# Scaling and turning the first four value heads on VectorE instead of TensorE and ScalarE

## The chip, the cores and the metric

The kernel runs on one core of a Trainium2 chip. The metric is the device time of one execution in microseconds (us), as a median of several runs. The engines are called PE (TensorE matmul), DVE (VectorE), ACT (ScalarE), POOL (GpSimd) and SP (SyncE, which here only issues DMAs). L405 means line 405 of the kernel before.

## The reference

One layer of a streaming encoder, in fp32, on 512 new prompt frames and 64 new sample frames (T = 576 rows in all). What matters here is its first stage: a norm, one wide projection, and the value heads that come out of it.

```python
hn = rmsnorm(x, g_norm1)                    # every row divided by its root mean square
proj = hn @ w_in                            # (576, 2048) @ (2048, 6144)
q, k, v, gb, gc, hc = jnp.split(proj, ...)  # 8 heads x 128 each for q, k, v; 1024 conv channels each for gb, gc, hc
...
o_attn = stick_breaking_blocks(q, k_all, v_all, P)
u = gc * hc                                 # then a convolution of width 3, times gb
...
x = x + mix @ w_out
x = x + (silu(h2 @ w_gate) * (h2 @ w_up)) @ w_down
```

`v` is an output too (`v_prompt`, `v_sample`), with the frame as row and the channel as column.

## The kernel before

**Layout.** All activations are kept with the channel on the 128 partitions and the 576 frames along the free axis. The row norm of `x` is not applied to `x`: the products run on `x * g_norm1`, and each result is multiplied later by `R1`, a [128, 576] tile that holds the factor of every frame, the same in all partitions. The same factors stand once more in `rst`, a [128, 5] tile with the frame on the partition.

**Stages.** First `x` is turned to the channel layout, and the value heads 0 to 3 are computed meanwhile with plain products (`step0`, L691); their sums go, not yet scaled, into the tiles `e0` (heads 0 and 1; names `E00`, `E01`) and `e1` (heads 2 and 3; name `E1`). The end of this is near 68 us. Then stage A does the other 22 units of `w_in`, then come the convolution and attention, the output projection and the feed-forward part.

**Units and products.** From stage A on, a unit is a 2048 x 256 block of a weight. It is done as seven products of half-size blocks (a Strassen-Winograd scheme), numbered 1 to 7; (3, 1) is product 1 of unit 3. A product is 24 matmuls of 128x128 by 128x288 in a row at L405: eight blocks, each with high part times high part, low times high and high times low. In stage A unit 0 and 1 are `gh` (convolution), unit 2 is `qk`, unit 3 is `gb`. PE runs the products in the order of the list `opening`, and then of a loop:

```python
opening = [(0, 1), (0, 2), (1, 1), (0, 3), (0, 6), (1, 2), (0, 5), (0, 7), (1, 3), (0, 4), (1, 6), (2, 1), (1, 5),
           (1, 7), (2, 2), (1, 4), (2, 6), (2, 7), (2, 5)]      # then (3, 1), (2, 3), (2, 4), (3, 2), ...
```

**What a product needs.** The weight block arrives by DMA in `raw_a` or `raw_b` (L328, 1 MB each). DVE forms sums of its quarters in place (L345, L349, L351, L353), ACT rounds the block to its high part (`whl`, L228), and DVE subtracts to get the low part (`whl`, L229). Four `whl` tiles go round, so the split for a product can start only when the product four places earlier is done. The first matmul of a product needs ACT's half, the second needs DVE's. Behind products 1, 5 and 6 ACT keeps a copy of the running sum (`part`, L428), and DVE adds it to another product's sum later (L897, L919, L931).

**Order of the work.** PE runs in the order of the program. DVE, ACT, POOL and SP are ordered by a list scheduler from stage A on, which places the instructions by its own idea of when their inputs are there; on the chip each engine then runs its list strictly in order. A small queue of generators (`pipe`) decides where on PE's list, and how early, the side work is written: one tick passes per three matmuls, and `yield n` puts the rest n ticks later.

**The four heads.** `plain_tokens` (spawned at L975, with lags of 8, 22, 36 and 50 ticks) takes one of the four `E` tiles: PE turns four 128x128 pieces (L790) and the last 64 frames (L798), ACT copies them from PSUM with the factor of `rst` as scale (L793, L800), and SP stores each piece twice, to the output and to `v_dram`, from which attention reads later: four DMAs. The heads 4 and 5 use `tokens` (L804) instead: DVE turns the [128, 576] tile in 32x32 squares in one instruction (L807), and ten DMAs put the pieces, 128 bytes each, into their places (L812, L815). The tiles `tokp`, `toks` and `tok` come from three buffers under the tag `hl`, which `ghs`, `s2` and `yt` use too.

Of the kernel before, what the change touches and what calls it, by code (L numbers as in the profile page):

```python
# [12 lines left out]
AF = mybir.ActivationFunctionType  # L13
ALU = mybir.AluOpType
PSUM = bass.MemoryType.PSUM

P = 128
TP = 512
TS = 64
T = TP + TS  # L20
# [82 lines left out]
def tile_hybrid_stream_step(  # L103
# [6 lines left out]
    nc = tc.nc  # L110
# [6 lines left out]
    kp, vp, ks, vs = k_prompt[0, 0], v_prompt[0, 0], k_sample[0, 0], v_sample[0, 0]  # L117
# [18 lines left out]
    v_dram = tc.dram_tile([NH, T, P], F32, name="v_dram")  # L136
# [4 lines left out]
    def misc(name):  # L141
        return ps_z.tile([P, 512], F32, tag="misc", name=name, bufs=2)
# [75 lines left out]
    pipe = Pipeline()  # L218
# [18 lines left out]
    ident = const.tile([P, P], F32, name="ident")  # L237
# [277 lines left out]
    ssr, rst, nhalf = (vecs[:, o : o + 5] for o in (304, 312, 320))  # L515
# [14 lines left out]
    R1 = None  # L530
# [98 lines left out]
    def hl_tile(name):  # L629
        return tmp.tile([P, 2, HALF], F32, tag="hl", name=name, bufs=3).rearrange("p i t -> p (i t)")  # L630

    LAG = 3
    with tc.manual_schedule(engines={mybir.EngineType.Activation, mybir.EngineType.DVE, mybir.EngineType.SP}):
# [102 lines left out]
        R1 = rpool.tile([P, T], F32, tag="R", name="R1", bufs=2)  # L736
# [48 lines left out]

    def plain_tokens(E, h, lag):
        yield lag
        pa = misc("tok_p")
        for i in range(4):
            nc.tensor.transpose(pa[:, i * P : (i + 1) * P], E[:, i * P : (i + 1) * P], ident)  # L790
        t = hl_tile("tokp")[:, :TP].rearrange("p (i d) -> p i d", d=P)
        for i in range(4):
            nc.scalar.activation(out=t[:, i, :], in_=pa[:, i * P : (i + 1) * P], func=AF.Copy, scale=rst[:, i : i + 1])  # L793
        nc.sync.dma_start(out=vp[:, h, :].rearrange("(i p) d -> p i d", p=P), in_=t)
        nc.sync.dma_start(out=v_dram[h][:TP].rearrange("(i p) d -> p i d", p=P), in_=t)
        yield 3
        pb = misc("tok_q")
        nc.tensor.transpose(pb[:TS, :P], E[:, TP:T], ident)  # L798
        tz = hl_tile("toks")[:TS, :P]
        nc.scalar.activation(out=tz, in_=pb[:TS, :P], func=AF.Copy, scale=rst[:TS, 4:5])  # L800
        nc.sync.dma_start(out=vs[:, h, :], in_=tz)
        nc.sync.dma_start(out=v_dram[h][TP:], in_=tz)

    def tokens(E, dst, dst_s, dram, lag):  # L804
        yield lag
        t = hl_tile("tok")
        nc.vector.transpose(out=t, in_=E)  # L807
        for g in range(0, P, BK):
            rows = t[g : g + BK].rearrange("j (t c) -> j t c", c=BK)
            for b, to in ((TP, dst), (T, dram)):  # L810
                if to is not None:
                    nc.sync.dma_start(out=to[:, g : g + BK].rearrange("(t j) c -> j t c", j=BK),  # L812
                                      in_=rows[:, : b // BK])
        for a in range(TP, T, BK):
            nc.sync.dma_start(out=dst_s[a - TP : a - TP + BK].rearrange("j (g c) -> g j c", c=BK), in_=t[:, a : a + BK])  # L815
# [158 lines left out]
    for E, h, lag in ((e1[0], 2, 8), (e1[1], 3, 22), (e0[0], 0, 36), (e0[1], 1, 50)):  # L974
        pipe.spawn(plain_tokens(E, h, lag))  # L975
# [111 lines left out]
    for h in range(NH):  # L1087
        t = tpool.tile([P, 2, T], F32R, tag=f"t{h}", name=f"mixa{h}")
# [658 lines left out]
```

## Time and the profile before

| | |
|---|---|
| median of 3 runs | 2322.34 us (2322.25 to 2322.53) |
| the profiled execution | 2323.28 us, its span 2321.6 us |
| PE busy | 2310.5 us (100% of the span) |
| DVE busy | 1952.7 us (84%) |
| ACT busy | 1216.2 us (52%) |
| POOL busy | 303.7 us (13%) |
| DMA moved | 368.57 MB, 159 GB/s on average |

Times in the trace count from the start of the span. A timeline row gives the start, the duration, the engine, the line, the operation, out<-in and the count, and in brackets how long the engine had been idle and what ended that. A row's duration is from its start to its end, while the engine starts the next one a little earlier; so what an instruction costs on a busy engine is the step from its start to the next start.

### The profile page before, as it was taken

The numbers are of one execution on the slowest core, as the hardware profiler recorded it, in microseconds if no ns is written. First come the engines' busy times: TensorE is split into PE (matmuls) and PEld (weight loads), VectorE is DVE, ScalarE is ACT, GpSimd is POOL, SyncE is SP. The second block draws the span as 40 slices with busy tenths as digits, with TensorE's granted clock in tenths as the row PEclk, the third lists the DMA queues.
The fourth block names the chain that finished last, engine by engine and source line by source line (L and its number), as shares of the span: only waits on it lengthen the run. The fifth ranks groups of instructions, "written<-read, shape, count | busy, mean of one in ns | idle before, by whom it ended". The sixth has DMA issues, their size and how long they took to land.

```text
span 2321.6 us, 43509 instructions
## 1 busy us (share of the span) xinstructions
PE 2310.5 (100%) x17404; PEld 2303.5 (99%) x17404; DVE 1952.7 (84%) x2878; ACT 1216.2 (52%) x2163; POOL 303.7 (13%) x374
## 2 busy tenths in 40 slices
PE   9999999999999999999999999999999999999999
PEld 8999999999999999999999999999999999999999
DVE  8889989897778898888888888888888777987897
ACT  8556656455787554444444444444444444444443
POOL 0212121110332320000000000000000002431222
PEclk9999999999999999999999999999999999999999
DMA  8444343546754554544444444344344936885654
GB/s 273 134 121 130 89 145 101 153 122 208 194 142 120 179 189 127 158 149 129 155 130 150 141 139 155 119 152 152 121 155 136 351 129 208 226 242 186 207 128 109
DMA packets 544762, 368.57 MB, mean 159 GB/s; under 512 B 84918, under 2 KB 528976, under 8 KB 544560
## 3 DMA queue, kind: packets, MB, share of 16 engines
q1 hardware_dynamic: 538064, 356.42, 49.2%
q0 software_dynamic: 6384, 9.24, 2.3%
q8 instruction: 136, 2.23, 0.4%
q14 instruction: 66, 0.54, 0.1%
q10 hardware_dynamic: 112, 0.14, 0.0%
HBM read 285.52 MB, written 80.23 MB: 158 GB/s over the span
## 4 chain that ended last, share of the span: by engine, by line
PE 94%; DVE 2%; ACT 2%; POOL 1%; DMA 1%; issue 0%; SPq 0%; POOLq 0%; ACTq 0%; DVEq 0%
PE psy L405 47%; PE psw L405 24%; PE psx L405 12%; PE pjo L224 5%; PE pj L691 1%; PE pjz L691 1%; PE psv L405 1%; PE pjm L691 1%; DVE wlo L177 0%; DVE pl L229 0%; PE psx L556 0%; DMA vtok<-v_dram 0%; ACT ph L228 0%; ACT pr L1237 0%; DVE z L1235 0%
## 5 line engine op out<-in xcount | busy, mean ns | idle before, releaser
L229 DVE TENSOR_TENSOR whl<-raw_a,whl 128x1024 fp32r<-128x1024 f32 (+4 forms) x384 | 431.7, 1125 | 55.7 <-ACT whl L228 54.2
L405 PE MATMUL psy<-t,whl 128*128 128x288 f32 x3000 | 447.1, 294 | 0.0
L228 ACT CAST whl<-raw_a 128x1024 fp32r<-128x1024 f32 (+4 forms) x384 | 360.4, 940 | 139.0 <-PE psx L405 42.8
L405 PE MATMUL psy<-h_s,whl 128*128 128x288 f32 x2766 | 416.4, 294 | 0.0
L405 PEld LDWEIGHTS psy<-t,whl 128*128 128x128 f32 x3000 | 414.4, 188 | 0.0
L405 PE MATMUL psw<-t,whl 128*128 128x288 f32 x2688 | 388.9, 294 | 0.0
L405 PEld LDWEIGHTS psy<-h_s,whl 128*128 128x128 f32 x2766 | 383.1, 188 | 0.1
L405 PEld LDWEIGHTS psw<-t,whl 128*128 128x128 f32 x2688 | 366.8, 188 | 0.0
L228 ACT CAST whl<-raw_b 128x1024 fp32r<-128x1024 f32 (+5 forms) x234 | 211.3, 905 | 206.9 <-issue 71.3
L229 DVE TENSOR_TENSOR whl<-raw_b,whl 128x1024 fp32r<-128x1024 f32 (+5 forms) x234 | 252.0, 1077 | 72.9 <-ACT whl L228 72.1
L428 ACT COPY part<-psy 128x288 f32<-128x288 f32 x309 | 122.9, 398 | 340.2 <-PE psy L405 337.8
L405 PE MATMUL psx<-h_s,whl 128*128 128x288 f32 x1164 | 170.2, 294 | 0.0
L228 ACT CAST whl<-s 128x1024 fp32r<-128x1024 f32 (+5 forms) x103 | 95.3, 925 | 123.2 <-PE psw L405 115.6
L405 PEld LDWEIGHTS psx<-h_s,whl 128*128 128x128 f32 x1164 | 159.6, 188 | 0.0
L405 PE MATMUL psy<-t12a,whl 128*128 128x288 f32 x1056 | 150.4, 295 | 0.0
L405 PE MATMUL psw<-t34a,whl 128*128 128x288 f32 x1056 | 150.4, 295 | 0.0
L405 PEld LDWEIGHTS psy<-t12a,whl 128*128 128x128 f32 x1056 | 143.3, 188 | 0.2
L405 PEld LDWEIGHTS psw<-t34a,whl 128*128 128x128 f32 x1056 | 143.5, 188 | 0.0
L1462 POOL DMA_DIRECT2D hid_dram<-form x7 | 5.2, 736 | 950.8 <-DVE form L229 943.7
L229 DVE TENSOR_TENSOR whl<-s,whl 128x1024 fp32r<-128x1024 f32 (+5 forms) x103 | 110.2, 1070 | 19.3 <-ACT whl L228 18.4
L224 PE MATMUL pjo<-mixc,whi 128*128 128x288 f32 x512 | 118.8, 299 | 0.0
L224 PE MATMUL pjo<-mixa,whi 128*128 128x288 f32 x512 | 102.8, 295 | 0.0
(566 smaller groups left out, 3915.7 us busy)
## 6 DMA issues: line engine op xcount, KB each, us to landing
hid_dram<-form SPq DMA_DIRECT2D x147, 288.0 KB
raw_a<-in_w_in_dram SPq DMA_DIRECT2D x22, 1024.0 KB
raw_b<-in_w_in_dram SPq DMA_DIRECT2D x22, 1024.0 KB
raw_b<-in_w_gate_dram SPq DMA_DIRECT2D x22, 1024.0 KB
raw_b<-in_w_up_dram SPq DMA_DIRECT2D x22, 1024.0 KB
raw_a<-in_w_gate_dram SPq DMA_DIRECT2D x22, 1024.0 KB
raw_a<-in_w_up_dram SPq DMA_DIRECT2D x22, 1024.0 KB
h_s<-hid_dram SPq DMA_DIRECT2D x10, 2016.0 KB
```

What stands on the lines that cost most here:

```text
L224: mm(ps, w_[:, k, csl], x_[:, a:b], start=(k == 0 and n == 0), stop=(k == nk - 1 and n == 2))
L228: cast = nc.scalar.copy(out=hi, in_=src)
L229: (lo_eng or nc.vector).tensor_tensor(out=lo, in0=src, in1=hi.bitcast(F32), op=ALU.subtract)
L405: mm(ps, whl[:, w_, j, :], x_, start=(start and j == 0 and q == 0), stop=(j == len(xs_) - 1 and q == 2), skip_group_check=True)
L428: nc.scalar.copy(out=t, in_=st["y"])
L691: mm(banks_[c][i], w3[:, kt % 8, c * P : (c + 1) * P], t[:, x_, :], start=(kt == 0 and n == 0), stop=(kt == KD - 1 and n == 2))
L1462: q.dma_start(out=hid_dram[fp][2 * n - 2 : 2 * n].rearrange("f p t -> p f t"), in_=t.bitcast(F32))
```

## The change

`plain_tokens` keeps its lags. Now DVE multiplies the whole `E` tile by `R1` in place, and `tokens` is spawned two ticks later, which turns the tile in 32x32 squares on DVE and issues ten DMAs. Twenty PE turns, twenty ACT copies and sixteen DMAs go; four multiplications [128, 576] and four square turns on DVE and forty DMAs come.

```diff
     def plain_tokens(E, h, lag):
         yield lag
-        pa = misc("tok_p")
-        for i in range(4):
-            nc.tensor.transpose(pa[:, i * P : (i + 1) * P], E[:, i * P : (i + 1) * P], ident)
-        t = hl_tile("tokp")[:, :TP].rearrange("p (i d) -> p i d", d=P)
-        for i in range(4):
-            nc.scalar.activation(out=t[:, i, :], in_=pa[:, i * P : (i + 1) * P], func=AF.Copy, scale=rst[:, i : i + 1])
-        nc.sync.dma_start(out=vp[:, h, :].rearrange("(i p) d -> p i d", p=P), in_=t)
-        nc.sync.dma_start(out=v_dram[h][:TP].rearrange("(i p) d -> p i d", p=P), in_=t)
-        yield 3
-        pb = misc("tok_q")
-        nc.tensor.transpose(pb[:TS, :P], E[:, TP:T], ident)
-        tz = hl_tile("toks")[:TS, :P]
-        nc.scalar.activation(out=tz, in_=pb[:TS, :P], func=AF.Copy, scale=rst[:TS, 4:5])
-        nc.sync.dma_start(out=vs[:, h, :], in_=tz)
-        nc.sync.dma_start(out=v_dram[h][TP:], in_=tz)
+        nc.vector.tensor_tensor(out=E, in0=E, in1=R1, op=ALU.mult)
+        pipe.spawn(tokens(E, vp[:, h, :], vs[:, h, :], v_dram[h], 2))
```

Lines below L785 move up by 13 (L807 becomes L794, L897 becomes L884, and so on). The scheduler makes a new order of DVE, ACT and SP out of it, for the next 35 products or so. Three places matter.

**DVE, while unit 0 and 1 run.** The numbers behind the names are tile numbers: before, `whl_1156` is the split for product (0, 7), `whl_1208` for (1, 3) and `whl_1240` for (0, 4). Before:

```order
L345 TENSOR_TENSOR s1_1203<-raw_b_960 128x1024 [waits DMAHW2_49,DVE_49]
L229 TENSOR_TENSOR whl_1156<-raw_b_960,whl_1156 128x1024 [waits Activation_49]
L349 TENSOR_TENSOR raw_b_960<-raw_b_960,raw_a_100 128x8x128 [waits DVE_49]
L351 TENSOR_TENSOR raw_a_100<-s1_1203,raw_a_100 128x8x128 [waits DVE_49]
L353 TENSOR_TENSOR raw_a_100<-raw_a_100 128x8x128 [waits DVE_49]
L229 TENSOR_TENSOR whl_1208<-raw_a_100,whl_1208 128x1024 [waits PE_49,Activation_49]
L919 TENSOR_TENSOR c_1236<-psx2_1211,part_1120 128x288 [waits PE_49]
L229 TENSOR_TENSOR whl_1240<-raw_b_960,whl_1240 128x1024 [waits Activation_49]
```

Of the change, at the same place, where `whl_1193` is the split for (1, 3) and `whl_1225` for (0, 4):

```order
L788 TENSOR_TENSOR E00_636<-E00_636,R1_653 128x576
L345 TENSOR_TENSOR s1_1188<-raw_b_960 128x1024 [waits DMAHW2_49,DVE_49]
L794 STREAM_TRANSPOSE tok_1171<-E00_636 128x576 [waits DVE_49]
L349 TENSOR_TENSOR raw_b_960<-raw_b_960,raw_a_100 128x8x128 [waits DVE_49]
L906 TENSOR_TENSOR c_1221<-psx2_1196,part_1104 128x288 [waits PE_49]
L351 TENSOR_TENSOR raw_a_100<-s1_1188,raw_a_100 128x8x128 [waits DVE_49]
L907 TENSOR_TENSOR c_1221<-c_1221,R1_653 128x288 [waits DVE_49]
L353 TENSOR_TENSOR raw_a_100<-raw_a_100 128x8x128 [waits DVE_49]
L229 TENSOR_TENSOR whl_1225<-raw_b_960,whl_1225 128x1024 [waits Activation_49]
L788 TENSOR_TENSOR E01_637<-E01_637,R1_653 128x576
L229 TENSOR_TENSOR whl_1193<-raw_a_100,whl_1193 128x1024 [waits Activation_49]
```

The split for (1, 3) now stands behind four multiplications and three turns (two multiplications and two turns came before this piece), and behind the split for (0, 4), which stood after it.

**DVE, at the end of unit 2.** Before, `whl_1597` is the split for (3, 1), `whl_1627` for (2, 3) and `whl_1667` for (2, 4); `part_1695` is ACT's copy behind product (2, 5):

```order
L229 TENSOR_TENSOR whl_1597<-raw_a_100,whl_1597 128x1024 [waits Activation_49]
L943 SCALAR_TENSOR_TENSOR c_1236<-u_1517,vec_109,c_1236 128x578 [waits Activation_49]
L351 TENSOR_TENSOR raw_a_100<-s1_1735,raw_a_100 128x8x128 [waits DVE_49]
L943 SCALAR_TENSOR_TENSOR c_1236<-u_1517,vec_109,c_1236 128x578 [waits DVE_49]
L229 TENSOR_TENSOR whl_1627<-raw_a_100,whl_1627 128x1024 [waits PE_49,Activation_49]
L229 TENSOR_TENSOR whl_1667<-raw_b_960,whl_1667 128x1024 [waits Activation_49]
L853 SCALAR_TENSOR_TENSOR yt_1650<-yt_1650,ss_1647 128x288 [waits Activation_49]
L854 SCALAR_TENSOR_TENSOR yt_1650<-yt_1650 128x288 [waits DVE_49]
L855 SCALAR_TENSOR_TENSOR E-20_1553<-E-20_1553,gqs_110,yt_1650 128x288 [waits DVE_49]
L897 TENSOR_TENSOR E-20_1697<-psw_1631,part_1695 128x288 [waits Activation_49]
```

Of the change, where `whl_1577` is the split for (3, 1), `whl_1607` for (2, 3), and `part_1675` is the copy behind (2, 5):

```order
L229 TENSOR_TENSOR whl_1607<-raw_a_100,whl_1607 128x1024 [waits Activation_49]
L930 SCALAR_TENSOR_TENSOR c_1221<-u_1497,vec_109,c_1221 128x578 [waits Activation_49]
L930 SCALAR_TENSOR_TENSOR c_1221<-u_1497,vec_109,c_1221 128x578 [waits DVE_49]
L840 SCALAR_TENSOR_TENSOR yt_1630<-yt_1630,ss_1627 128x288 [waits Activation_49]
L841 SCALAR_TENSOR_TENSOR yt_1630<-yt_1630 128x288 [waits DVE_49]
L842 SCALAR_TENSOR_TENSOR E-20_1533<-E-20_1533,gqs_110,yt_1630 128x288 [waits DVE_49]
L884 TENSOR_TENSOR E-20_1677<-psw_1611,part_1675 128x288 [waits Activation_49]
L886 TENSOR_TENSOR E-20_1677<-E-20_1677,R1_653 128x288 [waits DVE_49]
L229 TENSOR_TENSOR whl_1577<-raw_a_100,whl_1577 128x1024 [waits DMAHW5_49,Activation_49]
```

The split for (3, 1) has moved behind the addition that uses the copy behind (2, 5); before it stood nine instructions ahead of that addition.

**ACT, at the same place**, of the change only:

```order
L838 ACTIVATE yt_1630<-yt_1630 128x288 [waits Activation_49]
L839 ACTIVATE yt_1630<-yt_1630 128x288 [waits Activation_49]
L428 COPY part_1675<-psy_1405 128x288 [waits PE_49]
L228 CAST whl_1577<-raw_a_100 128x1024 [waits DMAHW5_49]
L228 CAST whl_1647<-raw_b_960 128x1024
```

ACT's half of the split for (3, 1) also stands right behind the copy after (2, 5), which waits for PE. On PE the products (2, 5) and (3, 1) follow each other in both kernels.

## The prediction

> **What bounds the kernel now.** I read the page's busy times and its chain first, then what PE waits for, then PE's timeline where the four heads are turned, then DVE's.
>
> ```profile
> PE 2310.5 (100%) x17404; PEld 2303.5 (99%) x17404; DVE 1952.7 (84%) x2878; ACT 1216.2 (52%) x2163; POOL 303.7 (13%) x374
> PE 94%; DVE 2%; ACT 2%; POOL 1%; DMA 1%; issue 0%; SPq 0%; POOLq 0%; ACTq 0%; DVEq 0%
> ...
> PE psx L556 <- DMA xin<-in_x_prompt_dram: 4.9, 2, 4.2
> PE psx L405 <- DVE whl L229: 0.2, 1, 0.2
> ...
> 68.00:94.00 26.00, 26.00 (x200) 25.74 (x199) 23.05 (x27) 17.03 (x37) 1.70 (x2) 1.00 0.53 151
> 94.00:120.00 26.00, 26.00 (x198) 26.00 (x197) 21.46 (x27) 10.72 (x14) 11.88 (x15) 1.00 0.50 145
> ```
>
> PE bounds the kernel: it is busy all the time, and the chain of work that ended last is PE's for 94%. At the matmuls of the units (L405) it waited for DVE once, 0.2 us. So whatever PE no longer does is gained in full, and whatever makes PE wait is lost in full. In the stretch of the change (the two windows: width, then busy PE, weight load, DVE, ACT, POOL, granted clock, DMA share, GB/s) DVE is busy for 89% and 83%. It is the engine that gets more work, with little room.
>
> **What PE saves.** PE's timeline around the third head, and two products further on:
>
> ```profile
> 83.35 2.14 PE L405 MATMUL psy<-t12a,whl 128*128 128x288 f32 x15
> 85.33 0.60 PE L790 MATMUL tok_p<-ident,E 128*128 128x128 f32 x4
> 85.68 1.47 PE L405 MATMUL psy<-t12a,whl 128*128 128x288 f32 x9
> 86.99 0.27 PE L798 MATMUL tok_q<-ident,E 128*64 128x128 f32 x1
> 87.02 3.45 PE L405 MATMUL psx<-bod,whl 128*128 128x288 f32 x24
> 90.30 1.36 PE L405 MATMUL psy<-t12a,whl 128*128 128x288 f32 x9
> ...
> 94.07 3.37 PE L405 MATMUL psw<-t34a,whl 128*128 128x288 f32 x24
> 106.80 3.33 PE L405 MATMUL psy<-b,whl 128*128 128x288 f32 x24
> ```
>
> Four products lie between 94.07 and 106.80, so one is 3.18 us. The two products between 83.35 and 90.30 took 6.95 us, 0.59 more than 6.36: that is what five turns cost. Four heads make 2.4 us, all on the path. It is 0.1% of the run.
>
> **What DVE gets.** The trace has the same shapes:
>
> ```profile
> 71.50 1.22 DVE L349 TENSOR_TENSOR raw_b<-raw_b,raw_a 128x1024 f32<-128x1024 f32 x1
> 72.64 0.75 DVE L229 TENSOR_TENSOR t12a<-tab,t12a 128x576 fp32r<-128x576 f32 x1
> 73.31 1.21 DVE L351 TENSOR_TENSOR raw_a<-s,raw_a 128x1024 f32<-128x1024 f32 x1
> ...
> 159.87 0.77 DVE L807 STREAM_TRANSPOSE tok<-E-20_1697 128x576 f32<-128x576 f32 x1
> 160.57 0.47 DVE L969 SCALAR_TENSOR_TENSOR mc<-oc,vec,mc 128x288 fp32r<-128x288 f32 x1
> ...
> 82.30 1.23 DVE L229 TENSOR_TENSOR whl<-s,whl 128x1024 fp32r<-128x1024 f32 x1 [1.45 <-ACT whl L228]
> 90.69 1.23 DVE L229 TENSOR_TENSOR whl<-raw_a,whl 128x1024 fp32r<-128x1024 f32 x1 [1.11 <-ACT whl L228]
> 91.83 0.45 DVE L919 TENSOR_TENSOR c<-psx,part 128x288 f32<-128x288 f32 x1
> 92.20 1.22 DVE L229 TENSOR_TENSOR whl<-raw_b,whl 128x1024 fp32r<-128x1024 f32 x1
> ```
>
> From start to start, an operation on 128x576 takes 0.67 us, one on 128x1024 1.13, one on 128x288 0.37, a square turn 0.70. So a head costs DVE 1.37 us, four cost 5.5. ACT loses its twenty copies, which only frees it. PE waits for none of these; what counts is when the splits (L229) are ready.
>
> **First place: product (1, 3).** In the last fence the row at 90.69 is its split: ready at 91.92, wanted at 97.28, 5.4 us of cover. In the new order all of DVE's list from 71.50 on has its inputs early, so I add up its steps to the split of (1, 3): thirteen of 1.13 (14.7), six of 0.67 (4.0), three turns (2.1), four of 0.37 (1.5) and two small ones (some 0.4), together 22.7. The split then starts at 94.2 and is ready at 95.4. A cruder way gives the other end: 91.92, plus four multiplications and three turns (4.8), plus the split and two short operations now ahead of it (1.9), less the idle 1.1 of the row and 1.5 of the one above it, is 96.0. PE comes 2.4 us earlier and wants it with its second matmul at 95.0. It waits 0.4 to 1.0 us; I take 0.6, nearer to the step by step sum. (The split for (0, 3) is ready near 79.3 by the same steps, where PE wants it at 79.1; a wait of 0.2 there only shortens this one.) What may lengthen it is a POOL operation beside a DVE one:
>
> ```profile
> 110.99 2.20 DVE L353 TENSOR_TENSOR raw_a<-raw_a 128x1024 f32<-128x1024 f32 x1
> ```
>
> Sums of that size took 1.22 at 71.50. One such hit makes the wait up to 2.0; with every input a little earlier it is 0. Both ends go into the range.
>
> **Second place: product (3, 1).** This follows from the order alone. Before, PE ran (2, 5) and (3, 1) at the first two rows, and the split for (3, 1) (third row) was done 6 us ahead; the fourth row is ACT's copy behind (2, 5).
>
> ```profile
> 129.29 3.34 PE L405 MATMUL psy<-t12a,whl 128*128 128x288 f32 x24
> 132.47 3.33 PE L405 MATMUL psy<-b,whl 128*128 128x288 f32 x24
> ...
> 125.28 1.22 DVE L229 TENSOR_TENSOR whl<-raw_a,whl 128x1024 fp32r<-128x1024 f32 x1
> ...
> 132.67 0.40 ACT L428 COPY part<-psy 128x288 f32<-128x288 f32 x1 [1.70 <-PE psy L405]
> ```
>
> In the new order both halves of that split stand behind the copy: ACT's rounding right after it, DVE's subtraction after the addition that reads it. The copy waits for the last matmul of (2, 5), and PE's next product is (3, 1). So no slack can hide it: PE ends (2, 5), ACT copies, ACT rounds, DVE subtracts, and only then does the second matmul of (3, 1) run. The trace has this chain without anyone waiting, behind the product that ended as PE began its run at 94.07:
>
> ```profile
> 94.27 0.40 ACT L428 COPY part<-psy 128x288 f32<-128x288 f32 x1 [0.43 <-PE psy L405]
> 94.56 1.05 ACT L228 CAST whl<-raw_a 128x1024 fp32r<-128x1024 f32 x1
> 95.65 1.23 DVE L229 TENSOR_TENSOR whl<-raw_a,whl 128x1024 fp32r<-128x1024 f32 x1
> ```
>
> From 94.07 to 96.88 is 2.8 us; one matmul (0.13) fits in between. The wait is 2.7 us. Behind it the cover is back: the splits for (2, 3) and (2, 4) stand before or right behind, and four 1.13 us sums ahead of (3, 6) meet three products of PE (9.5 us).
>
> Between the two places the closest is (2, 6): its split comes after a chain that starts with the end of (1, 7) and has four steps of 128x1024 and three short ones, some 5.5 us, against two products (6.35 us). It passes with 0.6 to 0.8 to spare; a stretched DVE step would cost up to 0.4, which I put into the upper end only.
>
> **SP and the DMAs.** Sixteen DMAs become forty, thirty of them in a row ahead of the next load of `raw_b`, ten more ahead of `raw_a`. Heads 4 and 5 show twenty of the new kind:
>
> ```profile
> 435.52 0.34 SPq L812 DMA_DIRECT2D out_dram<-tok  x1
> 447.96 0.42 SPq L328 DMA_DIRECT2D raw_a<-in_w_in_dram  x1
> ...
> 93.44 0.37 SPq L328 DMA_DIRECT2D raw_b<-in_w_in_dram  x1
> 98.62 0.54 SPq L328 DMA_DIRECT2D raw_a<-in_w_in_dram  x1
> ```
>
> That is 12.4 us, 0.62 each. The first turn ends near 79.9, so thirty are out at 98.5, and `raw_b` is loaded 5 us later than at 93.44. By the steps above its sum (L345) is now reached near 112.5, so the load has 14 us. `raw_a` goes out near 105.5 instead of 98.62, and is used at 131. Two DVE instructions wait for stores to land: the turn of the fourth head for the stores of the first, and `ghs` near 101.4 for those of the second, issued by 92.4. I count nothing for all this; the stores have 9 us before `ghs` would wait at all, the loads about 10.
>
> **The sum.** -2.4 + 0.6 + 2.7 = +0.9 us. The profiled execution, 2323.28 us, is 0.94 above the median; PE bounds both, so the difference carries over: 2322.34 + 0.9 = 2323.2 us. A measurement of this kernel can tell about 0.2%, 4.6 us, from no change, so this counts as the same.
>
> **Rivals.**
>
> *The gain stays.* If the split of (3, 1) were not late, by a wait that I have read wrongly, only the first term and a wait of 0 to 0.6 at (1, 3) remain: 2319.9 to 2320.5 us. For it speaks that DVE before never let PE wait over 0.2 us; against it the order of both engines. 7%.
>
> *The clock falls.* PE would stand for 2.7 us. At the start of the run, after it had waited 4.2 us, the first matmuls were 0.24 apart, not 0.13:
>
> ```profile
> 8.19 0.44 PE L691 MATMUL pj<-b,whi 128*128 128x288 f32 x1
> 8.43 0.44 PE L691 MATMUL pj<-b12a,whi 128*128 128x288 f32 x1
> 10.35 0.44 PE L691 MATMUL pjz<-b12a,whi 128*128 128x288 f32 x1
> ```
>
> Some 3.5 us at that pace lose 1.6 us: 2324.8 us. Here the stop is shorter and broken by the first matmul of (3, 1) after 1.5 us. 12%. [...]
>
> *The small stores hold DVE up.* The other side: `ghs` waits for the twenty stores of the first two heads. From `ghs` to the split of (1, 7) are 2.8 us, and PE wants that at about 111.4, so it decides if the stores land after 108.6, that is at over 1.43 us a store from 79.9 on. At 1.8 the twenty land at 115.9, and PE loses 7.3 us more: 2330.5 us, slower by 0.35%. Against it stand the 0.62 of heads 4 and 5, for it that they run beside a 1 MB load here, and these two windows, of the small stores and of 1 MB loads:
>
> ```profile
> 436.00:442.00 6.00, 6.00 (x48) 6.00 (x47) 5.03 (x8) 2.11 (x2) 0.00 (x0) 1.00 0.56 97
> 452.00:456.00 4.00, 4.00 (x33) 4.00 (x32) 3.64 (x3) 1.35 (x2) 1.37 (x1) 1.00 1.08 324
> ```
>
> Per DMA share the small stores move 173 GB/s, the loads 300. 9%. [...]
>
> **How the numbers follow.** The forecast has 70%, the gain that stays 7%, the clock 12%, the stores 9%; 2% remain for a gain over 4.6 us, for which I see no source, since PE loses only 2.4 us of work. The forecast's own range is -2.4 + 0 + 2.7 = +0.3 to -2.4 + 2.0 + 2.7 + 0.4 = +2.7, that is 2322.6 to 2325.0. With the clock's case on top of part of it, and part of the way to the first rival, I give 2321.6 to 2326.2; the first rival and the stores, 16%, and the 2% stay out. Faster by over 0.2%: 0.02. Same: 0.70 + 0.07 + 0.12 = 0.89. Slower: 0.09.
>
> **What would show it.** Right: PE's waits have a row of 2 to 3 us for `whl` at L405 near 131 us, with PE's product of unit 3 starting right behind DVE's subtraction, and a row of under 1 us near 95; up to 94 PE runs 2.2 to 2.4 us ahead of before; behind 135 every product stands about 1 us later than before. Wrong: no such wait near 131, matmuls 0.24 apart behind it, or `ghs` starting later than 108 us.

## The result, and the profile after

| | before | after |
|---|---|---|
| median, runs side by side | 2322.44 us (6 runs, 2321.5 to 2324.03) | 2329.62 us (6 runs, 2328.78 to 2331.55) |
| ratio | | 1.0031, 95% interval 1.0021 to 1.0041 |
| profiled execution, its span | 2323.28 us, 2321.6 us | 2328.97 us, 2327.2 us |

The change makes the kernel slower by some 7 us of the median, and 5.7 us between the two profiled executions. The forecast was +0.9 us, and its range ended at 2326.2 us: it was wrong.

The profile page after, busy times; then what PE waited for (us in total, times, longest), the rows of the units:

```profile
PE 2312.1 (99%) x17384; PEld 2303.5 (99%) x17384; DVE 1960.2 (84%) x2886; ACT 1212.2 (52%) x2143; POOL 301.9 (13%) x374
...
PE psw L405 <- DVE ghs L918: 2.8, 1, 2.8
PE psy L405 <- ACT whl L228: 1.4, 1, 1.4
PE psy L405 <- DVE whl L229: 0.9, 1, 0.9
...
PE psv L405 <- DVE whl L229: 0.4, 1, 0.4
```

Three of the four rows were forecast: 0.4 at (1, 3), and 1.4 with 0.9 at (3, 1). The first, 2.8 us for `ghs`, was not. PE does less (20 turns fewer) and yet is busy 1.6 us longer, which points to the clock. PE's timeline after, then the same products before, where they aren't shown yet:

```profile
91.93 3.33 PE L405 MATMUL psw<-t34a,whl 128*128 128x288 f32 x24
95.10 0.29 PE L405 MATMUL psv<-bod,whl 128*128 128x288 f32 x1
95.80 3.34 PE L405 MATMUL psv<-bod,whl 128*128 128x288 f32 x23 [0.40 <-DVE whl L229]
101.90 3.48 PE L405 MATMUL psw<-t34a,whl 128*128 128x288 f32 x24 [2.76 <-DVE ghs L918]
105.22 3.33 PE L405 MATMUL psy<-t12a,whl 128*128 128x288 f32 x24
...
130.88 3.34 PE L405 MATMUL psy<-t12a,whl 128*128 128x288 f32 x24
135.65 0.40 PE L405 MATMUL psy<-b,whl 128*128 128x288 f32 x1 [1.43 <-ACT whl L228]
136.91 4.84 PE L405 MATMUL psy<-b,whl 128*128 128x288 f32 x23 [0.86 <-DVE whl L229]
141.59 3.37 PE L405 MATMUL psy<-bod,whl 128*128 128x288 f32 x24
```

```profile
97.28 3.33 PE L405 MATMUL psv<-bod,whl 128*128 128x288 f32 x24
100.45 1.75 PE L405 MATMUL psw<-t34a,whl 128*128 128x288 f32 x12
...
135.64 3.33 PE L405 MATMUL psy<-bod,whl 128*128 128x288 f32 x24
```

At (1, 3) PE is 2.18 us ahead (95.10 against 97.28). From there to (0, 4) it needs 6.80 us, before 3.17: 3.63 more, of which 0.56 at (1, 3) (its second matmul comes 0.70 behind the first, not 0.14) and 3.07 at (0, 4), which could have begun near 98.8 (95.10 + 3.17 + 0.56). From (2, 5) to (3, 1) it is 4.77 against 3.18, 1.59 more; the second matmul of (3, 1) comes 1.26 behind the first, 1.13 more; and its other 23 matmuls take 4.84 us instead of some 3.2, 1.64 more. -2.18 + 3.63 + 1.59 + 1.13 + 1.64, and 0.14 behind (0, 4), are +5.95 at (2, 3): 141.59 against 135.64. The span ends 5.6 later.

Why `ghs` is late stands in the timelines of DVE and ACT after, and then of DVE before:

```profile
98.67 0.76 DVE L794 STREAM_TRANSPOSE tok<-E 128x576 f32<-128x576 f32 x1
100.25 1.23 DVE L229 TENSOR_TENSOR whl<-s,whl 128x1024 fp32r<-128x1024 f32 x1 [0.82 <-ACT whl L228]
101.39 0.45 DVE L918 TENSOR_TENSOR ghs<-psw,part 128x288 f32<-128x288 f32 x1
...
99.17 1.04 ACT L228 CAST whl<-s 128x1024 fp32r<-128x1024 f32 x1 [2.50 <-PE psv L405]
```

```profile
97.48 0.46 DVE L931 TENSOR_TENSOR ghs<-psw,part 128x288 f32<-128x288 f32 x1 [0.60 <-PE psw L405]
98.04 0.53 DVE L935 TENSOR_TENSOR u<-ghs,c 128x224 f32<-128x224 f32 x2
98.56 1.23 DVE L229 TENSOR_TENSOR whl<-raw_a,whl 128x1024 fp32r<-128x1024 f32 x1
101.73 1.23 DVE L229 TENSOR_TENSOR whl<-s,whl 128x1024 fp32r<-128x1024 f32 x1 [1.94 <-ACT whl L228]
```

`ghs` reads the sum of (0, 7) out of the PSUM bank `psw`, and (0, 4) writes into the same bank. Before, DVE had been idle for 0.6 us when PE ended (0, 7) near 97.4, and read it at once (97.48), with a whole product, (1, 3), to spare. After, `ghs` stands in DVE's list behind the fourth head's turn and behind a split (`whl<-s`, that of (1, 5)), whose ACT half waits until PE has done (1, 3) (the last row), since it goes into the `whl` tile that (1, 3) used. So PE ends (1, 3), ACT rounds, DVE subtracts, DVE reads `psw`, and only then may (0, 4) begin. `ghs` itself waits for no DMA: no idle time stands before it.

The clock, from the windows of the profile after (width, busy PE, weight load, DVE, ACT, POOL, granted clock, DMA share, GB/s):

```profile
102.00:104.00 2.00, 2.00 (x15) 2.00 (x16) 0.48 (x2) 0.00 (x0) 0.33 (x2) 1.00 1.04 309
...
136.00:138.00 2.00, 1.14 (x8) 1.09 (x8) 2.00 (x3) 2.00 (x4) 0.00 (x0) 0.92 0.00 0
138.00:140.00 2.00, 2.00 (x10) 2.00 (x10) 2.00 (x3) 0.16 (x1) 0.00 (x0) 0.50 0.35 96
140.00:142.00 2.00, 2.00 (x14) 2.00 (x13) 1.93 (x3) 0.21 (x1) 0.00 (x0) 0.73 1.10 323
```

Behind the stop at (3, 1) it falls to half: 0.08, 0.50 and 0.27 of 2 us are missing, 1.7 us. Behind the longer stop at (0, 4) it stays at 1.00.

### The profile page after: what moved, and what is told of

Read it like the earlier page. It is cut to its first block, busy times and chain, and to the rows that moved or that the text cites. A ratio compares the mean times of both kernels' runs of the same rounds, so it can differ in the third digit from the quotient of the medians.

```text
span 2327.2 us, 43484 instructions
## 1 busy us (share of the span) xinstructions
PE 2312.1 (99%) x17384; PEld 2303.5 (99%) x17384; DVE 1960.2 (84%) x2886; ACT 1212.2 (52%) x2143; POOL 301.9 (13%) x374
## 4 chain that ended last, share of the span: by engine, by line
PE 91%; DVE 4%; ACT 2%; DMA 1%; issue 1%; POOL 0%; SPq 0%; POOLq 0%; DVEq 0%; ACTq 0%
PE psy L405 47%; PE psw L405 24%; PE psx L405 12%; PE pjo L224 6%; DVE whl L229 1%; PE psv L405 0%; DMA xt_dram<-st 0%; DVE wlo L177 0%; ACT ph L228 0%; DVE pl L229 0%; DMA kf<-qk_dram 0%; PE z L1166 0%; PE po L1276 0%; DVE wlo L229 0%; ACT pr L1224 0%
## 5 line engine op out<-in xcount | busy, mean ns | idle before, releaser
L405 PE MATMUL psy<-t,whl 128*128 128x288 f32 x3000 | 447.1, 294 | 0.0
L405 PE MATMUL psy<-h_s,whl 128*128 128x288 f32 x2766 | 416.4, 294 | 0.0
L405 PEld LDWEIGHTS psy<-t,whl 128*128 128x128 f32 x3000 | 414.4, 188 | 0.0
L405 PE MATMUL psw<-t,whl 128*128 128x288 f32 x2688 | 388.9, 294 | 0.0
L405 PEld LDWEIGHTS psy<-h_s,whl 128*128 128x128 f32 x2766 | 383.1, 188 | 0.1
L405 PEld LDWEIGHTS psw<-t,whl 128*128 128x128 f32 x2688 | 366.8, 188 | 0.0
L405 PE MATMUL psx<-h_s,whl 128*128 128x288 f32 x1164 | 170.2, 294 | 0.0
L405 PEld LDWEIGHTS psx<-h_s,whl 128*128 128x128 f32 x1164 | 159.6, 188 | 0.0
L405 PE MATMUL psw<-t34a,whl 128*128 128x288 f32 x1056 | 150.5, 295 | 2.8 <-DVE ghs L918 2.8
L405 PE MATMUL psy<-t12a,whl 128*128 128x288 f32 x1056 | 149.6, 295 | 0.0
L405 PEld LDWEIGHTS psw<-t34a,whl 128*128 128x128 f32 x1056 | 143.2, 188 | 3.0 <-DVE ghs L918 3.0
L405 PEld LDWEIGHTS psy<-t12a,whl 128*128 128x128 f32 x1056 | 143.3, 188 | 0.2
```

Source lines behind the costliest of these rows:

```text
L405: mm(ps, whl[:, w_, j, :], x_, start=(start and j == 0 and q == 0), stop=(j == len(xs_) - 1 and q == 2), skip_group_check=True)
```

## Experiments

The theory: what costs is the order into which the scheduler puts DVE's and ACT's lists when forty small stores stand on SP; it makes two stops, and the clock falls behind one. First rival: DVE's extra work costs this in any order. Second rival: the small stores themselves slow the kernel, as traffic or as issues in a queue. Medians are beside runs of the kernel before on the same chip (2322.03 to 2322.35 us).

| kernel | median, us | ratio to before, 95% |
|---|---|---|
| `ghs` over `part` | 2338.98 | 1.0071, 1.0059 to 1.0084 |
| split for (3, 1) first | 2326.05 | 1.0017, 1.0008 to 1.0026 |
| both | 2335.78 | 1.0057, 1.0044 to 1.0071 |
| whole stores | 2320.96 | 0.9996, 0.9987 to 1.0005 |
| turns 28 places later | 2332.55 | 1.0044, 1.0031 to 1.0056 |
| 24 stores on POOL's queue | 2370.00 | 1.0204, 1.0190 to 1.0218 |
| before, without PE's turns | 2319.99 | 0.9991, 0.9982 to 1.0000 |
| 24 stores on ACT's queue, turns 16 later | 2326.89 | 1.0021, 1.0012 to 1.0029 |
| the same, turns 20 later | 2328.74 | 1.0031, 1.0019 to 1.0043 |
| 16 stores on ACT's queue, turns 12 later | 2321.55 | 0.9997, 0.9988 to 1.0006 |

**What the turns cost PE.** The kernel before without PE's turns, with `pa = E` and, for the last frames, `pb = E`:

```diff
-        pa = misc("tok_p")
-        for i in range(4):
-            nc.tensor.transpose(pa[:, i * P : (i + 1) * P], E[:, i * P : (i + 1) * P], ident)
+        pa = E
```

> The kernel before with PE's twenty turns left out: ScalarE scales and copies the first four values as they stand, so the stored rows are not turned. It measures what the turns cost PE by themselves. Both theories: 2.2 to 2.4 us less than before, 2319.8 to 2320.2 us, 0.9990 of before. If PE had been waiting elsewhere anyway, the gain would be smaller.

2319.99 against 2322.27 us: 2.28 (the interval of the ratio, 0.9982 to 1.0000, leaves room from 0 to 4 us). That is about what there is to gain.

**Whole stores.**

```diff
+        if whole:
+            nc.sync.dma_start(out=dst.rearrange("(i p) d -> p i d", p=P), in_=t[:, :TP].rearrange("p (i d) -> p i d", d=P))
+            ...
+            return
         for g in range(0, P, BK):
```

> The changed kernel with four whole stores per head, as before, in place of ten small ones; what lands in the stored rows is then not in the reference's layout, the rest of the work is the same. The order of before comes back by itself: ghs behind the split for (1, 6), the split for (3, 1) ahead of the addition. Theory (the order, which the scheduler makes from when it takes the stores to land): 2320.3 to 2320.9 us, as with both edits. First rival (DVE's extra work, which is all still there): 2326 us or more. Second rival (the traffic of the small stores): 2320.5 us here, but not with both edits.

2320.96 us, as the theory has it, with DVE's work unchanged: the page, the waits of PE at the units, and `ghs`:

```profile
PE 2308.8 (100%) x17384; PEld 2301.1 (99%) x17384; DVE 1959.0 (84%) x2886; ACT 1211.7 (52%) x2143; POOL 303.5 (13%) x374
...
PE psv L405 <- DVE whl L229: 0.7, 2, 0.4
...
98.40 0.45 DVE L924 TENSOR_TENSOR ghs<-psw,part 128x288 f32<-128x288 f32 x1
```

DVE is as busy as after (1959.0 against 1960.2 us), and at the units PE never waits over 0.4 us at a time. The first rival falls here. The second is open still: the small stores are gone too.

**The split for (3, 1) first.** The copy behind (2, 5) and the addition that uses it are told to stand behind the two halves of that split:

```diff
+                with tc.issue_after(ahead[3 - NA, 1][0]):
                     st["u4"] = kept("acc")
...
+                with tc.issue_after(ahead[3 - NA, 1][1]):
                     nc.vector.tensor_tensor(out=E[:, a:b], in0=ps, in1=part, op=ALU.add)
```

> The changed kernel, with the split for (3, 1) set ahead of the copy behind (2, 5) on ACT and ahead of the addition that reads it on DVE; nothing else is moved. Theory (the order): both waits at (3, 1) go, 2.3 us, and the half clock behind them, 1.6 us, with the 0.4 between them; the stop of 2.8 us at (0, 4) stays, and the clock does not fall behind it. 4.3 us less than the changed kernel, 2325.3 us, 1.0013 of before. If the clock had fallen for another reason than this stop: 2.7 us less, 2326.9 us, with the half clock still near 138. First rival (DVE's extra work): a new wait for a split within ten products behind (3, 1), 2328 to 2330 us. Second rival (the traffic of the stores): the split is late there anyway, since its data is, 2329 us.

2326.05 us, 3.6 less than after (2.2 between the profiled executions), with all forty stores on SP. Of the waits at (3, 1), 0.7 for DVE's half is left. In the profiled execution the clock now fell behind the stop at (0, 4), which is as long as it was after; PE's timeline, and the windows (L405 is L409 in this kernel, and `ghs` L930):

```profile
101.75 4.97 PE L409 MATMUL psw<-t34a,whl 128*128 128x288 f32 x24 [2.76 <-DVE ghs L930]
...
136.38 3.31 PE L409 MATMUL psy<-b,whl 128*128 128x288 f32 x23 [0.67 <-DVE whl L232]
```

```profile
102.00:104.00 2.00, 2.00 (x11) 2.00 (x11) 0.32 (x2) 0.00 (x0) 0.32 (x2) 0.55 1.05 305
104.00:106.00 2.00, 2.00 (x11) 2.00 (x11) 0.00 (x0) 0.00 (x0) 0.00 (x0) 0.59 1.24 266
```

**Is the fall of the clock tied to a place?** The change, and this last kernel, in one more execution each.

> The changed kernel once more, for its granted clock by stretches. If the clock falls behind a stop of this length always or never, the half clock stands again behind (3, 1) near 138 us and not behind (0, 4) near 102 us. If it is a matter of when the stop comes, it may stand behind either, both or none: each place costs 1.6 us, so 2327.4 to 2331 us.

> The kernel with the split for (3, 1) ahead of the copy once more, for its granted clock. One stop of 2.8 us at (0, 4). If such a stop always lets the clock fall in this kernel, it is near 0.55 from 102 to 106 us again, and the time is 2326 to 2327 us; if it is a matter of when the stop comes, the clock may stay at 1.00, and the time is 2324.5 to 2325.5 us.

2329.66 us: half clock behind (3, 1) again (0.63 and 0.52 from 138 to 142), none behind (0, 4). 2328.0 us: behind (0, 4) again (0.90, 0.50, 0.75 from 100 to 106); this execution is longer than expected, with a further wait of 1.0 us for ACT's `part`, far behind this stretch. So each kernel repeats itself in its two profiled executions, and the same stop of 2.76 us lowers the clock in one kernel and not in the other. But not in all its executions: one fall misses 1.7 of some 2326 us, 0.07%, so a run whose mean granted clock is 1.000 can't hold one, and 4 of the 11 runs of the split for (3, 1) first have 1.000. They are its four fastest, 2324.78 to 2325.90 us; the other seven have 0.999 and took 2326.01 to 2326.81. So the same kernel runs with and without a fall; what decides it stays open.

**`ghs` over `part`.**

```diff
-                t = hl_tile("ghs")[:, : b - a]
+                t = part
```

> The changed kernel, with ghs written over part instead of into a buffer of its own, so that it no longer has to follow the stores of the second head; DVE's list then has ghs ahead of the split that waits for product (1, 3). Theory (the order: two stops, and the clock behind the second): the stop of 2.8 us at product (0, 4) goes, the stop of 2.3 us at (3, 1) stays, with the clock near 0.5 behind it; 3.0 us less than the changed kernel, 2326.6 us, 1.0018 of before. First rival (DVE's 5.5 us of extra work cost this in any order): the stop comes up again at another split, 2329 to 2330 us. Second rival (the traffic of the small stores stretches whatever waits): the wait stays, since it was one for data, 2329 us.

The stop at (0, 4) goes as expected, the one at (3, 1) stays. But a new one of 9.3 and 1.7 us stands at (2, 6), with the clock near 0.5 from 126 to 138 us, and the time is 2338.98 us. That reads like the first rival, so DVE's and SP's timelines have to decide (first PE's row):

```profile
131.14 0.61 PE L405 MATMUL psy<-t12a,whl 128*128 128x288 f32 x1 [9.30 <-ACT whl L228]
...
113.28 0.46 DVE L907 TENSOR_TENSOR c<-c,R 128x288 f32<-128x288 f32 x1
115.53 0.46 DVE L918 TENSOR_TENSOR part<-psw,part 128x288 f32<-128x288 f32 x1 [1.79 <-PE psw L405]
...
118.70 0.46 DVE L884 TENSOR_TENSOR E-20_1530<-psx,part 128x288 f32<-128x288 f32 x1 [2.08 <-PE psx L405]
...
125.33 1.22 DVE L345 TENSOR_TENSOR s<-raw_b 128x1024 f32<-128x1024 f32 x1
...
100.49 0.41 SPq L328 DMA_DIRECT2D raw_b<-in_w_in_dram  x1
```

The sum at 125.33 needs a block whose load went out at 100.49; in its place in the list it stands behind instructions that wait for PE, product by product, while DVE idles. Before, the same sum ran 9.6 us after its load (93.44 to 102.99); here 24.8 us lie between. DVE had the time, and by that comparison the data; the order was bad. My expectation missed that one edit moves the whole list.

**Both edits.** The two diffs together.

> Both edits: ghs over part, and the split for (3, 1) ahead of the copy. Ten small stores per head stay, and DVE's extra work stays. Theory (the order): what is left is the 2.2 to 2.4 us of the turns less the 0.6 at (1, 3): 2320.5 to 2320.9 us, 0.9992 to 0.9994 of before, and no wait of over 1 us at the units. First rival (DVE's extra work): 2326 us or more, with new waits for splits. Second rival (the traffic of the stores): 2324 us or more, with waits that end with a DMA.

2335.78 us: no wait at (0, 4), none at (3, 1), and the same 9.3 and 1.7 us at (2, 6). As a way to the forecast 2320.5 us it failed, for the reason above.

**Forty small stores in a good order.** The next four keep the small stores and look for an order without stops: first by spawning the turns later, 28 ticks behind the multiplication in place of 2,

```diff
-        pipe.spawn(tokens(E, vp[:, h, :], vs[:, h, :], v_dram[h], 2))
+        pipe.spawn(tokens(E, vp[:, h, :], vs[:, h, :], v_dram[h], 28))
```

> The changed kernel with the turns of the four heads spawned 28 places later in place of 2; the same DVE work and the same forty small stores, all on SP. DVE's list then has ghs ahead of the split for (1, 3) and the split for (3, 1) ahead of the addition behind (2, 5); the sums for the units behind (3, 1) stand later than with whole stores. Theory (the order): neither stop, so no fall of the clock: 2320.3 to 2321.5 us, 0.9992 to 0.9996 of before, if the later sums cause no new wait. Rival (the traffic of the small stores): 2324 us or more, with waits that end with a DMA.

Neither stop is left, but there are two new ones (PE's timeline): 3.9 us at (1, 5), whose bank ACT's copy into `part` has to free, and 3.0 with 1.2 at (3, 6); behind each the clock falls, 1.7 us each.

```profile
111.53 4.99 PE L405 MATMUL psy<-t12a,whl 128*128 128x288 f32 x24 [3.92 <-ACT part L428]
...
151.82 0.40 PE L405 MATMUL psy<-t12a,whl 128*128 128x288 f32 x1 [2.98 <-ACT whl L228]
```

The copy overwrites the `part` that the second `ghs` reads, so it waits for `ghs`, which stands at 110.60 behind seven instructions of 128x1024 in a row; the other stop ends with a chain of sums that begins (L345) at 146.09, though its load was issued at 115.96. Again no wait ends with a DMA: order, not traffic. Then with 24 of the stores on another queue, POOL's (turns 16 later), or ACT's (turns 16, and 20 later):

```diff
-            for b, to in ((TP, dst), (T, dram)):
+            for b, to, q in ((TP, dst, nc.sync), (T, dram, nc.gpsimd)):        # or nc.scalar
                 if to is not None:
-                    nc.sync.dma_start(out=to[:, g : g + BK].rearrange("(t j) c -> j t c", j=BK),
+                    q.dma_start(out=to[:, g : g + BK].rearrange("(t j) c -> j t c", j=BK),
```

> The changed kernel with 16 of the forty small stores on SP, 24 on GpSimd's queue, and the turns spawned 16 places later in place of 2. DVE's list is then that of the kernel with whole stores at both places and behind them. Theory (the order): 2320.3 to 2321.0 us, 0.9992 to 0.9995 of before, and no wait of over 1 us at the units. Rival (the traffic of the small stores): 2324 us or more. What could come on top: GpSimd issuing 24 DMAs beside DVE could stretch some of DVE's work; that would show as waits for whl of up to 1 us.

2370 us. I was wrong by far about POOL: its timeline shows one store every 2.3 us or more, and between and behind them multiplications by `R1` that DVE needs. DVE's operations on 128x1024 were not stretched beside these issues: 1.18 to 1.23 us from 106 to 138.

```profile
113.34 0.67 POOL L799 DMA_DIRECT2D v_dram<-tok  x1 [1.79 <-issue]
115.84 0.69 POOL L802 DMA_DIRECT2D out_dram<-tok  x1 [1.83 <-issue]
...
133.94 0.80 POOL L908 TENSOR_TENSOR c<-c,R 128x288 f32<-128x288 f32 x1
```

Here `ghs` did wait for stores to land, 8.15 us, up to 106.15.

> The changed kernel with 24 of the forty small stores (the scratch copy and the last rows) on ScalarE's queue, 16 on SP, and the turns spawned 16 places later in place of 2. DVE's list is then that of the kernel with whole stores at all the places that stopped PE so far: both ghs early, the split for (3, 1) ahead of the addition, the sums for the units behind (3, 1) early. Same DVE work, same forty stores, same bytes. Theory (the order): 2320.3 to 2321.2 us, 0.9991 to 0.9995 of before, no wait of over 1 us at the units. Rival (the small stores themselves, here their issue on ScalarE, some 0.55 us each, six in a row, ahead of a cast): waits for whl or part that end with ScalarE, 2323 us or more.

> As the one with 16 places, with the turns 20 places later. The stores stand apart in ScalarE's list, six between two casts; on DVE both ghs stand one behind the other, ahead of two splits. Theory (the order): 2320.3 to 2321.2 us, unless the second ghs, which waits for product (0, 4) to end, holds up the splits behind it by one product (3.2 us): then 2323 to 2325 us. Rival (the small stores themselves): as there, 2323 us or more, with waits that end with ScalarE.

2326.89 and 2328.74 us: the second rival, in the form of issues. With 16, PE waits once, 4.3 us, for a copy that stands on ACT behind eleven stores; ACT's queue and ACT:

```profile
84.10 1.49 ACTq L799 DMA_DIRECT2D v_dram<-tok  x3
85.62 2.96 ACTq L802 DMA_DIRECT2D out_dram<-tok  x2
88.68 2.32 ACTq L799 DMA_DIRECT2D v_dram<-tok  x4
91.04 1.67 ACTq L802 DMA_DIRECT2D out_dram<-tok  x2
92.75 0.40 ACT L428 COPY part<-psy 128x288 f32<-128x288 f32 x1 [8.26 <-DMA v_dram<-tok]
```

The 4.3 us, and the clock (0.53, 0.50, 0.50, 0.77 from 92 to 100), at which the product behind the stop took 5.85 us in place of 3.17 (93.20 to 99.05), are the 7 us over the time without turns. With 20 the stop is 4.0 us, with another of 0.8 at (1, 3); ahead of the copy that PE waits for stand six issues, of which four took 8.9 us (ACT's queue in that kernel), two casts and an activation:

```profile
100.73 8.91 ACTq L799 DMA_DIRECT2D v_dram<-tok  x4
```

Why these took so long stays open. DVE's list makes no stop in either. The last kernel therefore puts only four stores of a head on ACT, and no two heads' in a row:

```diff
+                    q = nc.scalar if to is dram and g in (64, 96) else nc.sync
+                    q.dma_start(out=to[:, g : g + BK].rearrange("(t j) c -> j t c", j=BK),
```

> The changed kernel with four of a head's ten small stores on ScalarE's queue (two of the scratch copy, the last rows), six on SP, and the turns spawned 12 places later in place of 2. DVE's list has both ghs early, the split for (3, 1) ahead of the addition and the sums behind it early; on ScalarE no two heads' stores stand one behind the other, so at most four issues, some 2.2 us, lie ahead of a copy or cast. Same DVE work, same forty stores. Theory (the order, and what an issue costs the queue that it stands in): 2320.3 to 2321.5 us, 0.9991 to 0.9996 of before, no wait of over 1 us at the units. Rival (the small stores cost this in whatever queue): a wait for part or whl of 2 us or more that ends with ScalarE, 2324 us or more.

2321.55 us against 2322.35 of before beside it. The page, PE's waits at the units, and `ghs` (L919 here):

```profile
PE 2309.4 (100%) x17384; PEld 2301.8 (99%) x17384; DVE 1960.6 (84%) x2886; ACT 1212.7 (52%) x2143; POOL 305.4 (13%) x374
...
PE psv L405 <- DVE whl L229: 0.8, 2, 0.6
PE psy L405 <- ACT part L428: 0.4, 1, 0.4
...
98.59 0.45 DVE L919 TENSOR_TENSOR ghs<-psw,part 128x288 f32<-128x288 f32 x1
```

Same forty stores, same DVE work, no stop, no fall of the clock: 8 us less than the change as it was made. It does what the change meant to do, but whether it beats the kernel before can't be told (0.9988 to 1.0006); some 2.3 us are to be had.

## Why the prediction was wrong

- **What PE saves, -2.4:** right. -2.18 at (1, 3), 2.28 without turns.
- **First place, (1, 3), 0.6:** right, 0.56. The split was ready at 95.74, where the sum over DVE's steps gave 95.4. That it fits so well is in part luck: one split on the way (92.11, the next row at 93.86) took 1.75 us in place of 1.13, with a POOL multiplication beside it from 91.13 to 92.85, and the rest of the list came 0.3 early. (Beside the 2.20 us at 110.99 that the prediction shows stood POOL's L946, from 109.97 to 113.35. In the profile before 20 of DVE's rows on 128x1024 take over 1.5 us, all of them with a POOL row beside them (as 56 shorter ones have), and none of the 652 without one does.)
- **Second place, (3, 1), 2.7:** right, 1.59 + 1.13 = 2.72, by the chain that the prediction followed. That this stop comes from the order is shown by the kernel that undoes it.
- **(2, 6) passes:** right; and the sums and the two later loads (at 100.05 and 109.43, forecast 98.5 and 105.5) kept nobody waiting.
- **SP and the DMAs, "I count nothing for all this": this step failed.** It worked out that `ghs` comes near 101.4, and it came at 101.39. It asked what `ghs` waits for, the stores, and there it was right. Of what waits for `ghs` it looked, in the rival of the small stores, only at the splits behind it in DVE's list. It missed the bank: PE's next product into `psw`, (0, 4), could have begun near 98.8 and may not until `ghs` has read. 3.07 us at (0, 4), with 0.14 behind it, were on the path from the forecast's own number. Whole stores, the turns 28 later and four stores of a head on ACT have the same DVE work, the last two also the same forty stores, and none has this stop: the order makes it.
- **The clock falls, 12%, +1.6:** the price was right (1.64), the chance too low: each of the four profiles of the change and of the split for (3, 1) first has one fall. The 3.5 us at half pace in that price were my estimate, and no row of the profile before shows them: at the start of the run, which I took for comparison, the matmuls are 0.24 apart from 7.95 to 10.59, 2.64 us, and the granted clock there is 1.00. In their place the profile after has 0.50 from 137.7 to 141.1, 3.4 us, which makes the 1.7 us missing. I held against a fall that the stop is shorter than the 4.2 us that PE stood there, and broken: 1.43 and 0.86 us, with a matmul in between, were enough twice. One stop of 2.76 us had both outcomes, by its clock also within one kernel, and how long PE must stand for the clock to fall no run here shows. The ends of two runs differ as well: in the profile after the clock falls near 2325.6 (1.00 up to there, 0.50 from 2325.8), some 2.7 us behind the end of PE's last matmul (2322.88); in the profile before it stays at 1.00 to the end of the span, 4.1 us behind PE's last (2317.52).
- **The small stores hold DVE up, 2330.5:** near the measured median by chance. `ghs` was not later than 108 and waited for no store; that mechanism appeared only with stores on POOL's queue.

The forecast's +0.9, with 3.2 for the missed stop and 1.64 for the clock, is 5.7: the difference of the two profiled executions. The medians differ by 1.5 us more. 0.84 of it is the profiled execution of before, which lies above its median. For the rest, a second fall of the clock in some executions would do: the two longest of the six runs (2331.55 and 2330.59 us) have a mean granted clock of 0.998, the others 0.999. But the mean also counts the end of the run, where PE is done and the clock can fall (0.50 from 2325.8 us in the profile after), and no profile of the change shows a second fall, so this is not shown.

## What to carry to other kernels

When a change moves instructions in a list that an engine runs strictly in order, go through every instruction that got later and ask who waits for it, not only what it waits for: here the next product into a PSUM bank began at 101.90, when DVE had read the bank (101.39, 0.45 us). In this kernel a stop of PE of 2.3 us or more cost its own length and, in most of the profiles, 1.6 us or more of half clock on top. And the small DMAs were paid where they were issued: they delayed what stood behind them in that queue (on ScalarE eleven of them stood ahead of a copy for which PE waited 4.3 us), and moved what the scheduler orders by its idea of when they land.

## What the runs showed of the hardware that was not expected

- TensorE's granted clock fell to half behind a stop of 1.43 and 0.86 us, broken by one matmul; behind 2.76 us it fell in one kernel (in both profiles, but by the mean clock not in 4 of 11 runs) and not in another (in neither of two profiles). One fall misses 1.7 us of clock, also behind stops of 3.9 and 4.0 us; behind one of 4.3 us it was 3.4 us.
- GpSimd issued the small stores 2.3 us apart or more, and what stood behind them on it came that much later; SP, in the change, took 5.7 to 8.9 us for the ten of a head, 0.57 to 0.89 each.
- Four such stores on ScalarE's queue took 2.3 us in one place and 8.9 us in another.
